# A whole-row first load, two copies on VectorE and new planned landings in a matmul-tanh-multiply kernel

## The chip, the cores and the metric

The kernel runs on one core of one Trainium2 chip. The metric is the device time of one execution in microseconds (us), as the median of several runs.

## The reference

```python
batch, m, k, n = 16, 512, 1024, 768
y1 = np.matmul(x, w1)        # x: (16, 512, 1024) float32, w1 and w2: (1024, 768) float32
y2 = np.matmul(x, w2)
return (np.tanh(y1) * y2).astype(np.float32)
```

Both products share x. Flattened, x has 8192 rows, which are 64 row tiles of 128.

## The kernel before, in words

**Tiling.** Rows go in tiles of 128 (mt 0 to 63). The inner dimension of 1024 is 8 slices of 128 (k), in two halves of 4 (h = 0, 1). The 768 columns of each weight are a block of F = 512 and a block of G = 256; "a" is w1's 512 columns, "b" w2's 512, "g" the 256 columns of both side by side. Operands are cast to float16, products accumulate in float32 in eight PSUM banks.

**Two ways to multiply.** The first four row tiles (HEAD = 4) are multiplied plainly: for each tile and block, eight matmuls m{mt}{s}{k}, for instance m0a0, over the slices in the order in which the weights land. The other 60 tiles go in triples i = 0 to 19. Three tiles by two halves against two halves by three blocks are multiplied with 15 products p0.i to p14.i of four matmuls each; in exchange there are sums of x blocks (S...), of weight blocks (B..., made once) and of partial results (copy, seed, add). Then tanh on ScalarE (t, th) and a product on VectorE (m, mh) give the output. Tile 3 keeps its b block for the end, where its 16 matmuls of 256 columns (m3y...) fill waits of TensorE.

**Getting x transposed.** TensorE needs x with the inner dimension on the partitions. The first seven tiles are transposed on TensorE itself: PT{mt}{h} is four 128 x 128 transposes of one half into a PSUM bank, and e{mt}{h} (evacuate, L383) copies the bank into the float16 tile xT, on ScalarE or VectorE. The halves named in FP32, (0, 0) and (1, 0), are transposed as float32 straight from the loaded tile; the others are first cast to float16 on VectorE, cx{mt}{h} (cast_x). Later tiles are loaded by GpSimd's queue and transposed by DMA from SyncE's queue.

**The first loads.** ScalarE's queue issues a0 to a3, the first four slices of w1 (load_w). SyncE's queue issues, in the order of the list on_sp (L530), the x halves (x00 is half 0 of tile 0), more slices of w1 and then the g slices, each 256 KB. GpSimd's queue issues the b slices and further x tiles (by_pool), behind a gate that waits for the cast cg0 of the first g slice. Casts of weight slices are ca{k} on VectorE, cg0 on VectorE, cg1 to cg7 on ScalarE. The loads of SyncE and ScalarE share eight completion semaphores in turn, so a load is issued only when the one eight places ahead of it has landed.

**What keeps TensorE going at the start.** WARM (L250) is a row of matmuls on constants, issued ahead of everything. FILL is 512 + 512 + 256 columns of the same kind; f0warm and f1warm put one FILL behind PT00 and one behind PT10.

**Who sets the order.** No loop order is written out. Each operation is declared with the engines that may do it and its cost there, a due time, what it needs, and for loads the time at which it will land (lands, LANDING). The class Planner runs these through a list schedule and gives each engine its fixed instruction order; the order of the 15 products (PE_ORDER, strict) is given. So a change of a planned cost, landing or start moves instructions on every engine, all through the kernel. START and P7 (L510, L511) place the triples' products in planned time, lands (L535) and now (L536) the first landings.

**Elsewhere.** D{mt} sums |x| of a tile on ScalarE, for a range flag that is tested at the end (a general path follows if it fails). Stores go out from SyncE's queue, st{mt}; that of tiles 0 and 2 waits for a late product and goes whole, tile 1's in two parts.

Of the kernel before, what the change touches and what calls it, by code (L numbers as in the profile page):

```python
# [74 lines left out]
class Planner:  # L75
# [151 lines left out]
def kernel(  # L227
# [7 lines left out]
    nc = tc.nc  # L235
# [4 lines left out]
    KH = KO // 2  # L240
# [3 lines left out]
    HEAD = 4  # L244
    TRIPLES = (MT - HEAD) // 3
    BY_PE = HEAD + 3
    FP32 = ((0, 0), (1, 0))
    LOW, HIGH = 512.0, 1024.0
    XT_BUFS, XH_BUFS, S_BUFS, O_BUFS, C_BUFS = 12, 8, 2, 9, 2
    WARM = 512, 512, 512, 512, 512, 512, 512  # L250
    FILL = 512, 512, 256
    FREE = 3
    TURNS = (2, 0, 1), (0, 2, 1)
    LANDING = {7: 35.9, 9: 37.2, 8: 39.4, 10: 47.4, 11: 48.3, 12: 49.2, 13: 55.0, 14: 56.3, 15: 57.6}
    rows = list(range(HEAD)) + [HEAD + 3 * i + r for i in range(TRIPLES) for r in (TURNS[i] if i < len(TURNS) else (0, 1, 2))]
    turn = {mt: n for n, mt in enumerate(rows)}
    S_AHEAD, HALVED = 4.0, 4
# [4 lines left out]
    xf = x.flatten_outer_dims().rearrange("(mt p) k -> mt p k", p=P)  # L262
# [8 lines left out]
    banks = [pspool.tile([P, F], f32, name=f"bank{i}") for i in range(8)]  # L271
# [21 lines left out]
    x_first = [early_x[:, mt * K:(mt + 1) * K] for mt in range(HEAD)]  # L293
# [38 lines left out]
    def half(h):  # L332
        return slice(h * KH * P, (h + 1) * KH * P)

    def constants(out, cols):
        fixed = ones.bitcast(bf16)
        pin(nc.tensor.matmul(out[:, :cols], fixed[:, :P], fixed[:, 1:2].to_broadcast([P, cols]), start=True, stop=True))
# [5 lines left out]
    def x_staged(mt, h):  # L343
        return x_first[mt][:, half(h)] if mt < HEAD else arena[:, STAGED * F:(STAGED + 1) * F]

    def load_first(e, mt, h):
        pin(nc.sync.dma_start(x_staged(mt, h), xf[mt][:, half(h)]))

    def cast_x(e, mt, h):
        copy(e, xh(mt)[:, half(h)], x_staged(mt, h))  # L350
# [156 lines left out]
    SLOT = KH * MM  # L507
    CAST = {"a": {"dve": 0.37}, "g": {"act": 0.495}, "g0": {"dve": 0.37}}
    FINE = (5, 36, 37, 45)
    START = 28.6  # L510
    P7 = 13.0  # L511
    ORIGIN = START - 6 * SLOT

    position = {}
# [12 lines left out]

    XX = 1.4
    LAG_FROM, LAG = 21.5, 1.2
    on_sp = "x00 x10 x20 x30 x01 x60 x11 a4 a5 x21 a6 x31 a7".split() + [f"g{k}{t}" for k in range(KH) for t in range(2)]  # L530
    by_pool = "b0 b4 b1 b5 x61 x4 b2 x51 x50 b6 b3 b7".split()
    GATES = {"b0": ("cg0", w_cols("g", 0)[:, :1])}
    arrivals = on_sp[4:] + by_pool
    size = {"x": 0.68, "a": 0.68, "g": 0.75, "b": 0.63}
    lands = dict(zip("x00 a0 x10 a1 x20 a2 x30 a3".split(), (4.31, 4.47, 6.13, 6.53, 7.7, 8.17, 9.05, 9.44)))  # L535
    now = 9.2  # L536
    for n in arrivals:
        now += 1.25 if n in by_pool and n[0] == "x" and len(n) == 2 else size[n[0]]
        lands[n] = now + (LAG if now > LAG_FROM else 0.0)

    for k in range(4):
        op(f"La{k}", {"act": 0.45}, -100, [], load_w, "a", k, issued=[f"La{k - 1}"] if k else [], lands=lands[f"a{k}"])
    for n, what in enumerate(on_sp):
        before = [f"L{on_sp[n - 1]}"] if n else []
        if what[0] == "x":
            op(f"L{what}", {"sp": 0.05}, 0.1 * n - 100, [], load_first, int(what[1]), int(what[2]), issued=before, lands=lands[what])
        else:
            s, k = what[0], int(what[1])
            j = slices.index((s, k))
            js = range(j, j + 1 + (s == "g"))  # L550
            old = [f"c{a}{b}" for a, b in (slices[i - SLOTS] for i in js if i >= SLOTS)] + [f"cx{HEAD + 2}0"] * (STAGED in js)
            op(f"L{what}", {"sp": 0.05}, 0.1 * n - 100, [], load_w, s, k, int(what[2]) if s == "g" else None, issued=before,
               behind=old, lands=lands[what])
    op(f"cx{HEAD + 2}0", {"dve": 0.37}, lands["x60"] - 1, ["Lx60"], cast_x, HEAD + 2, 0,
       behind=[f"cx{m}{h}" for m in range(2, HEAD) for h in range(2) if xh_place(m) == xh_place(HEAD + 2)])
    issued, x_loads = [], {(HEAD + 2, 0): (f"cx{HEAD + 2}0", lands["x60"])}
# [30 lines left out]
    def by_pe(mt, h, due, load):  # L587
        fp32 = (mt, h) in FP32
        op(f"PT{mt}{h}", {"pe": 0.44 if fp32 else 0.24}, due, [load], transpose_pe, mt, h, ("T", mt, h), chains=[("T", mt, h)])
        op(f"e{mt}{h}", {"dve": 0.6 if fp32 else 0.45, "act": 0.5} if mt < HEAD else {"act": 0.5}, due + 0.4, [f"PT{mt}{h}"], evacuate, mt, h, ("T", mt, h),  # L590
           chains=[("T", mt, h)])

    for n, after in enumerate(("PT00", "PT10")):
        op(f"f{n}warm", {"pe": 0.54}, -50, [after], fill, ("f", n), chains=[("f", n)])
    for mt in range(HEAD):
        for h in range(2):
            if (mt, h) not in FP32:
                op(f"cx{mt}{h}", {"dve": 0.37}, lands[f"x{mt}{h}"] - 1, [f"Lx{mt}{h}"], cast_x, mt, h)
            by_pe(mt, h, lands[f"x{mt}{h}"] - 2, f"Lx{mt}{h}" if (mt, h) in FP32 else f"cx{mt}{h}")
        op(f"D{mt}", {"act": 1.05}, START + 8, [f"Lx{mt}0", f"Lx{mt}1"], abs_x, mt, hold=11 + 4 * mt)  # L600
    for mt in rows[HEAD:BY_PE]:
        for h in range(2):
            by_pe(mt, h, x_loads[mt, h][1] - 2 - 0.1 * h * (mt == HEAD + 1), x_loads[mt, h][0])
# [152 lines left out]
    for mt in range(MT):  # L756
        i = (mt - HEAD) // 3 if mt >= HEAD else -1
        if mt < HEAD:
            kept = mt == HEAD - 1
            for t in range(2 if mt == 1 else 0):  # L760
                op(f"st{mt}{'ag'[t]}", {"sp": 0.05}, 1e3, outs[mt][t:t + 1], store, mt, t * F, (F, G)[t], behind=[f"p12.{11 + 2 * mt}"], xfer=0.5)
            if mt != 1:
                op(f"st{mt}", {"sp": 0.05}, 1e3, outs[mt][:1] if kept else outs[mt], store, mt, F if kept else 0, G if kept else N, behind=[f"p12.{11 + 2 * mt}"], xfer=1.0)
            for t in range(2 if kept else 0):
                op(f"st{mt}{chr(88 + t)}", {"sp": 0.4, "act": 0.4}, 2e4, outs[mt][1 + t:2 + t], store, mt, t * G, G, xfer=0.4)
            continue
        late = [f"{('p0', 'p4', 'p11')[(mt - HEAD) % 3]}.{i + 1}"] if i < TRIPLES - 2 else []
        if i == TRIPLES - 1:
            for a, lo, n in ((0, 0, F), (1, F, G)):
                part = outs[mt][a:a + 1]  # L770
                op(f"st{mt}{a}", {"sp": 0.4, "act": 0.4}, 2e4, part, store, mt, lo, n, xfer=0.4)
        else:
            op(f"st{mt}", {"sp": 0.05}, slot_of[max(i, 0), "p2"] + 12, outs[mt], store, mt, behind=late, xfer=1.0)
# [28 lines left out]
    soon = {"L" + n for n in on_sp[:4]} | {f"La{k}" for k in range(4)}  # L802
    pin(nc.vector.memset(ones, 2.0 ** -12))
    for n, cols in enumerate(WARM):
        constants(banks[n], cols)
    for n in sorted(soon, key=lambda n: plan.start_of[n]):
        o = plan.ops[n]
        o["fn"](plan.engine_of[n], *o["args"])
# [107 lines left out]
```

## Time and profile before

| | |
|---|---|
| median of 3 runs | 297.45 us (297.3 to 297.87) |
| profiled execution, its own time | 297.16 us |
| its span in the profile | 295.6 us |
| TensorE busy | 289.5 us |
| VectorE busy | 255.8 us |
| ScalarE busy | 224.4 us |
| GpSimd busy | 42.3 us |
| HBM read, written | 39.85 MB, 25.17 MB |

The span runs from the first recorded instruction to the last; the execution's time has some 1.6 us more around it. In the rows that follow PE is TensorE's matmul side, PEld its weight load, DVE VectorE, ACT ScalarE, POOL GpSimd, SP SyncE; a q behind a name is the engine's instruction queue. A row of the order of time has the start and the duration in us, the engine, the source line, the operation, what it writes and reads, how many were merged (x4), and in brackets how long the engine had been idle and what ended that.

### The profile page before, as it was taken

Reading aid. Unit: us, or ns where it says so; the run is one execution under the profiler, and the core shown is the slowest. Engines: PE = TensorE matmul, PEld = TensorE weight load, DVE = VectorE, ACT = ScalarE, POOL = GpSimd, SP = SyncE. Lnnn points to the kernel's source line nnn. Section 1 sums busy time; section 2 is a strip of 40 time slices with the busy share of each in tenths; the row PEclk is TensorE's granted clock in tenths of the full one; section 3 lists DMA queues with packets and bytes.
Section 4 is the critical chain, followed back from the end, with each engine's and each line's share of the span. In section 5 each row is a group of like instructions: output and inputs, shape, how many; then the busy total and the mean of one; then the engine's idle time right before and its main releaser. Section 6 shows DMA issues by size and latency. Waiting matters only on the chain. (4 is left out here: it accounts for less than half of the span.)

```text
span 295.6 us, 4588 instructions
## 1 busy us (share of the span) xinstructions
PE 289.5 (98%) x1374; PEld 132.3 (45%) x1374; DVE 255.8 (87%) x552; ACT 224.4 (76%) x454; POOL 42.3 (14%) x94
## 2 busy tenths in 40 slices
PE   7999999999999999999999999999999999999994
PEld 3445444444444444444444444444444444444442
DVE  1679999999989998898989888898988889898875
ACT  2698599799878878877888888677777767778442
POOL 0065022202102102202012021020211100000000
PEclk9999999999999999999999999999999999999999
DMA  6999999999999999989999999999999999241234
GB/s 217 391 321 204 182 141 169 210 247 230 240 194 197 247 226 216 252 218 239 204 190 246 231 236 270 164 271 264 224 298 225 213 175 324 104 162 53 109 136 169
DMA packets 84858, 63.63 MB, mean 215 GB/s; under 512 B 62816, under 2 KB 67168, under 8 KB 84832
## 3 DMA queue, kind: packets, MB, share of 16 engines
q1 hardware_dynamic: 73888, 45.10, 59.7%
q0 software_dynamic: 9936, 16.65, 36.0%
q10 hardware_dynamic: 1008, 1.57, 1.5%
q8 instruction: 11, 0.18, 0.2%
q14 instruction: 15, 0.12, 0.1%
HBM read 39.85 MB, written 25.17 MB: 220 GB/s over the span
## 5 line engine op out<-in xcount | busy, mean ns | idle before, releaser
L457 PE MATMUL bank<-b,early_x 128*128 128x512 f16 x640 | 148.3, 379 | 0.0
L457 PEld LDWEIGHTS <-early_x 128*128 128x128 f16 x800 | 78.1, 98 | 94.3 <-DVE early_x L421 0.3
L467 DVE TENSOR_TENSOR bank<-bank,arena 128x512 f32<-128x512 f32 x100 | 69.6, 696 | 13.6 <-ACT arena L461 10.9
L461 ACT ACTIVATE arena<-bank 128x512 f32<-128x512 f32 x100 | 57.6, 596 | 18.1 <-PE bank L457 18.1
L475 DVE TENSOR_TENSOR o<-o,bank 128x256 f32<-128x256 f32 (+1 forms) x128 | 61.9, 516 | 7.3 <-ACT o L470 5.9
L390 ACT ACTIVATE junk<-xh 128x1024 f16<-128x1024 f16 x60 | 63.4, 1057 | 0.1
L457 PEld LDWEIGHTS <-xT 128*128 128x128 f16 x400 | 39.0, 98 | 46.9 <-issue 0.4
L457 PE MATMUL bank<-b,xT 128*128 128x512 f16 x240 | 58.3, 379 | 0.0
L470 ACT ACTIVATE o<-bank 128x256 f32<-128x256 f32 (+1 forms) x80 | 34.8, 438 | 26.0 <-DVE bank L467 22.8
L457 PE MATMUL bank<-wh,xT 128*128 128x512 f16 x160 | 41.0, 379 | 0.0
L457 PE MATMUL bank<-wh,early_x 128*128 128x512 f16 x160 | 40.9, 379 | 0.0
L362 POOL DMA_DIRECT2D xh<-in_x_dram x61 | 32.4, 540 | 16.6 <-ACT junk L390 8.6
L421 DVE TENSOR_TENSOR early_x<-early_x,xT 128x512 f16<-128x512 f16 x80 | 33.5, 420 | 0.5
L470 ACT ACTIVATE o<-arena 128x512 f32<-128x512 f32 x40 | 25.2, 629 | 7.5 <-DVE arena L467 7.5
L501 POOL CAST held<-xT 128x1 f32<-128x1 f16 x18 | 4.5, 251 | 161.3 <-DMA xT<-xh 161.3
L461 ACT ACTIVATE bank<-bank 128x512 f32<-128x512 f32 x40 | 21.4, 570 | 4.7 <-PE bank L457 3.9
L430 PE MATMUL bank<-wh,xT 128*128 128x512 f16 x72 | 19.5, 379 | 0.3
L467 DVE TENSOR_TENSOR arena<-bank,arena 128x512 f32<-128x512 f32 x20 | 13.7, 686 | 3.6 <-ACT arena L461 3.6
L421 DVE TENSOR_TENSOR early_x<-xT,xT 128x512 f16<-128x512 f16 x40 | 16.7, 418 | 0.0
L421 DVE TENSOR_TENSOR early_x<-xT,early_x 128x512 f16<-128x512 f16 x40 | 16.7, 418 | 0.0
L467 DVE TENSOR_TENSOR bank<-arena,bank 128x512 f32<-128x512 f32 x20 | 13.8, 692 | 0.1
L390 ACT ACTIVATE junk<-wh 128x768 f16<-128x768 f16 x16 | 13.6, 847 | 0.1
(51 smaller groups left out, 140.0 us busy)
## 6 DMA issues: line engine op xcount, KB each, us to landing
out_dram<-o SPq DMA_DIRECT2D x59, 384.0 KB, 5.1
xh<-in_x_dram POOLq DMA_DIRECT2D x58, 256.0 KB, 6.7
arena<-in_w_dram SPq DMA_DIRECT2D x12, 256.0 KB, 5.6
early_x<-in_x_dram SPq DMA_DIRECT2D x8, 256.0 KB, 4.9
arena<-in_w_dram ACTq DMA_DIRECT2D x4, 256.0 KB, 5.9
wh<-in_w_dram POOLq DMA_DIRECT2D x8, 128.0 KB, 5.5
xT<-xh SPq DMA_TRANSPOSE x57, 4.2
out_dram<-o SPq DMA_DIRECT2D x3, 256.0 KB, 2.5
```

The lines of the kernel that those rows point to most:

```text
L362: pin(nc.gpsimd.dma_start(xh(mt)[:, cols], xf[mt][:, cols]))
L390: pin(nc.scalar.activation(junk[:, :src.shape[-1]], src, ACT.Abs, scale=scale, accum_out=sums[:, column:column + 1]))
L421: pin(engine[e].tensor_tensor(x_operand(i, v), x_operand(i, a), x_operand(i, b), OP[how]))
L430: pin(nc.tensor.matmul(bank(chain)[:, :rhs.shape[-1]], xt(mt)[:, k, :], rhs, start=first, stop=k == KO - 1, skip_group_check=True))
L457: pin(nc.tensor.matmul(place(i, dst), x_operand(i, a)[:, k, :], w_rhs(b, k), start=begins and k == 0, stop=k == KH - 1, skip_group_check=T ...
L461: pin(nc.scalar.activation(place(i, dst), place(i, src), ACT.Copy, scale=float(sign)))
L467: pin(nc.vector.tensor_tensor(place(i, dst), a, b, ALU.add if signs == (1, 1) else ALU.subtract))
L470: pin(nc.scalar.activation(out_tile(HEAD + 3 * i + r)[:, lo:lo + n], place(i, src)[:, :n], ACT.Tanh, scale=float(sign)))
L475: pin(nc.vector.tensor_tensor(o, o, place(i, src)[:, at:at + n], ALU.mult))
L501: pin(nc.gpsimd.tensor_copy(held, xt(mt)[:, 0, :1]))
```

## The change

- Tile 0 of x is loaded by one DMA in whole rows (x0, 512 KB) instead of the halves x00 and x01; x01's place in the list of SyncE's loads falls away.
- WARM becomes nine matmuls of 512 columns and one of 128, and wraps over the eight banks. The fill behind PT00 goes, the one behind PT10 stays.
- The planned landings of the first eight loads are replaced, those of the rest are counted on from a later base with one load fewer. START, P7 and four entries of LANDING are lowered by 0.1 to 0.5.
- The copy e20 may go only to VectorE; for the other copies of the first four tiles ScalarE's planned cost is 0.6 instead of 0.5.
- Tile 0's store becomes two stores, like tile 1's.

The order that comes out of the planner: PT01 stands right behind PT00, with its cast first on VectorE; e01 and e20 are VectorE's, e31 ScalarE's; D1, D2 and D3 stand later on ScalarE, D1 behind cg7; cg4 stands ahead of tha0; m0g5 stands one place earlier. Between 30 and 280 us TensorE's order is the same, while adds and multiplies of VectorE and some copies and tanhs of ScalarE trade places. In the last triple p5, p4, p13 and p14 stand ahead of the first piece of tile 3's b block, and on VectorE the add60 ahead of the last but one triple's mh0. GpSimd's order is the same.

```diff
-    WARM = 512, 512, 512, 512, 512, 512, 512
+    WARM = 512, 512, 512, 512, 512, 512, 512, 512, 512, 128
-    LANDING = {7: 35.9, 9: 37.2, 8: 39.4, 10: 47.4, 11: 48.3, 12: 49.2, 13: 55.0, 14: 56.3, 15: 57.6}
+    LANDING = {7: 35.9, 9: 37.2, 8: 39.0, 10: 47.2, 11: 48.1, 12: 49.0, 13: 55.0, 14: 56.3, 15: 57.6}
...
     def load_first(e, mt, h):
-        pin(nc.sync.dma_start(x_staged(mt, h), xf[mt][:, half(h)]))
+        if h is None:
+            pin(nc.sync.dma_start(x_first[mt], xf[mt]))
+        else:
+            pin(nc.sync.dma_start(x_staged(mt, h), xf[mt][:, half(h)]))
...
-    START = 28.6
-    P7 = 13.0
+    START = 28.4
+    P7 = 12.5
...
-    on_sp = "x00 x10 x20 x30 x01 x60 x11 a4 a5 x21 a6 x31 a7".split() + [f"g{k}{t}" for k in range(KH) for t in range(2)]
+    on_sp = "x0 x10 x20 x30 x60 x11 a4 a5 x21 a6 x31 a7".split() + [f"g{k}{t}" for k in range(KH) for t in range(2)]
...
-    lands = dict(zip("x00 a0 x10 a1 x20 a2 x30 a3".split(), (4.31, 4.47, 6.13, 6.53, 7.7, 8.17, 9.05, 9.44)))
-    now = 9.2
+    lands = dict(zip("x0 a0 x10 a1 x20 a2 x30 a3".split(), (4.65, 4.87, 6.2, 6.55, 7.92, 8.12, 9.25, 9.45)))
+    now = 9.5
     for n in arrivals:
         now += 1.25 if n in by_pool and n[0] == "x" and len(n) == 2 else size[n[0]]
         lands[n] = now + (LAG if now > LAG_FROM else 0.0)
+    lands["x00"] = lands["x01"] = lands["x0"]
...
-        op(f"e{mt}{h}", {"dve": 0.6 if fp32 else 0.45, "act": 0.5} if mt < HEAD else {"act": 0.5}, ...
+        op(f"e{mt}{h}", {"dve": 0.45} if (mt, h) == (2, 0) else {"dve": 0.6 if fp32 else 0.45, "act": 0.6} if mt < HEAD else {"act": 0.5}, ...
...
-    for n, after in enumerate(("PT00", "PT10")):
-        op(f"f{n}warm", {"pe": 0.54}, -50, [after], fill, ("f", n), chains=[("f", n)])
+    op("fwarm", {"pe": 0.54}, -50, ["PT10"], fill, ("f", 0), chains=[("f", 0)])
...
-            for t in range(2 if mt == 1 else 0):
+            for t in range(2 if mt < 2 else 0):
...
-            if mt != 1:
+            if mt > 1:
...
-        constants(banks[n], cols)
+        constants(banks[n % len(banks)], cols)
```

More of the change, by code (lines that the diff above doesn't have):

```diff
@@ L545 @@
         if what[0] == "x":
-            op(f"L{what}", {"sp": 0.05}, 0.1 * n - 100, [], load_first, int(what[1]), int(what[2]), issued=before, lands=lands[what])
+            op(f"L{what}", {"sp": 0.05}, 0.1 * n - 100, [], load_first, int(what[1]), int(what[2]) if what[2:] else None, issued=before, lands=lands[what])
         else:
@@ L589, in by_pe, with x_load @@
         op(f"PT{mt}{h}", {"pe": 0.44 if fp32 else 0.24}, due, [load], transpose_pe, mt, h, ("T", mt, h), chains=[("T", mt, h)])
-        op(f"e{mt}{h}", {"dve": 0.6 if fp32 else 0.45, "act": 0.5} if mt < HEAD else {"act": 0.5}, due + 0.4, [f"PT{mt}{h}"], evacuate, mt, h, ("T", mt, h),
+        op(f"e{mt}{h}", {"dve": 0.45} if (mt, h) == (2, 0) else {"dve": 0.6 if fp32 else 0.45, "act": 0.6} if mt < HEAD else {"act": 0.5}, due + 0.4, [f"PT{mt}{h}"], evacuate, mt, h, ("T", mt, h),
            chains=[("T", mt, h)])
-    for n, after in enumerate(("PT00", "PT10")):
-        op(f"f{n}warm", {"pe": 0.54}, -50, [after], fill, ("f", n), chains=[("f", n)])
+    def x_load(mt, h):
+        return f"Lx{mt}" if f"x{mt}" in on_sp else f"Lx{mt}{h}"
+    op("fwarm", {"pe": 0.54}, -50, ["PT10"], fill, ("f", 0), chains=[("f", 0)])
     for mt in range(HEAD):
@@ L597 @@
             if (mt, h) not in FP32:
-                op(f"cx{mt}{h}", {"dve": 0.37}, lands[f"x{mt}{h}"] - 1, [f"Lx{mt}{h}"], cast_x, mt, h)
-            by_pe(mt, h, lands[f"x{mt}{h}"] - 2, f"Lx{mt}{h}" if (mt, h) in FP32 else f"cx{mt}{h}")
-        op(f"D{mt}", {"act": 1.05}, START + 8, [f"Lx{mt}0", f"Lx{mt}1"], abs_x, mt, hold=11 + 4 * mt)
+                op(f"cx{mt}{h}", {"dve": 0.37}, lands[f"x{mt}{h}"] - 1, [x_load(mt, h)], cast_x, mt, h)
+            by_pe(mt, h, lands[f"x{mt}{h}"] - 2, x_load(mt, h) if (mt, h) in FP32 else f"cx{mt}{h}")
+        op(f"D{mt}", {"act": 1.05}, START + 8, sorted({x_load(mt, h) for h in range(2)}), abs_x, mt, hold=11 + 4 * mt)
     for mt in rows[HEAD:BY_PE]:
```

## The prediction

> **What bounds the kernel now.** I read the page's busy times first, then PE's waits, then the windows, then the order of time in three places: the first 10 us, the stretch from 17 to 25 us, the last 12 us.
>
> ```profile
> PE 289.5 (98%) x1374; PEld 132.3 (45%) x1374; DVE 255.8 (87%) x552; ACT 224.4 (76%) x454; POOL 42.3 (14%) x94
> ```
> ```profile
> PE bank L337 <- DVE ones L803: 1.3, 1, 1.3
> PE bank L380 <- DMA early_x<-in_x_dram: 0.2, 1, 0.2
> ```
> ```profile
> 4.60:6.33 1.73, 1.52 (x7) 1.04 (x8) 0.43 (x1) 0.59 (x1) 0.00 (x0) 1.00 0.88 300
> 6.33:9.54 3.21, 3.05 (x17) 1.44 (x18) 1.41 (x4) 1.17 (x2) 0.00 (x0) 1.00 1.05 405
> 31.40:283.97 252.57, 252.57 (x1172) 114.44 (x1172) 228.41 (x489) 200.06 (x409) 33.15 (x72) 1.00 0.99 210
> ```
>
> (In the windows the columns are the stretch, its length, the busy time of PE, PEld, DVE, ACT and POOL, the granted clock, the DMA share and GB/s.) PE is the bound and it never rests: the list of its waits holds 1.5 us, all before 5 us, and in the window from 31.40 to 283.97 it is busy for the whole 252.57 us. Products and their order there are nearly untouched by the change. So the time is PE's start, plus a fixed stream, plus what is lost before 31 us and after 284 us. Only the two ends can pay.
>
> A busy PE hides short waits, because a matmul's shown time is longer than its step: in the rows of the end below, eight 512-column matmuls start at 286.37 and the next instruction at 288.10, so one step is 0.216 us. I therefore read starts, not busy times.
>
> ```profile
> 1.30 3.17 PE L337 MATMUL bank<-ones 128*128 128x512 bf16 x7 [1.30 <-DVE ones L803]
> 4.67 0.98 PE L380 MATMUL bank<-ident,early_x 128*128 128x128 f32 x4 [0.21 <-DMA early_x<-in_x_dram]
> 5.49 0.71 PE L337 MATMUL bank<-ones 128*128 128x512 bf16 x3
> 6.33 0.39 PE L430 MATMUL bank<-wh,xT 128*128 128x512 f16 x1
> 6.56 0.60 PE L380 MATMUL bank<-ident,early_x 128*128 128x128 f32 x4
> 6.99 0.71 PE L337 MATMUL bank<-ones 128*128 128x512 bf16 x3
> 7.54 0.90 PE L430 MATMUL bank<-wh,xT 128*128 128x512 f16 x3
> 8.47 0.40 PE L380 MATMUL bank<-ident_h,xh 128*128 128x128 f16 x4
> 17.43 0.38 PE L430 MATMUL bank<-wh,xT_kept 128*128 128x512 f16 x1
> 17.66 0.59 PE L430 MATMUL bank<-wh,xT 128*128 128x512 f16 x2
> 24.62 1.67 PE L430 MATMUL bank<-wh,xT 128*128 128x512 f16 x7
> ```
> ```profile
> 4.73 0.43 DVE L368 CAST wh<-arena 128x512 f16<-128x512 f32 x1 [2.92 <-DMA arena<-in_w_dram]
> 5.69 0.59 ACT L366 CAST xT<-bank 128x512 f16<-128x512 f32 x1 [1.53 <-PE bank L380]
> 7.98 0.43 DVE L368 CAST xh<-early_x 128x512 f16<-128x512 f32 x1 [0.74 <-DMA early_x<-in_x_dram]
> 15.98 0.42 DVE L368 COPY xT_kept<-bank 128x512 f16<-128x512 f16 x1
> 17.18 0.43 DVE L368 CAST wh<-arena 128x512 f16<-128x512 f32 x1 [0.78 <-DMA arena<-in_w_dram]
> ```
>
> What to see: the head is a chain from landing to cast to PE. The first g slice is cast at 17.18 as it lands and is ready at 17.61; its matmul m0g0 starts at 17.66. The four fp32 transposes take 0.82 us the first time (4.67 to 5.49) and 0.43 the second (6.56 to 6.99); the 1280-column fill takes 0.55 (6.99 to 7.54). So PE's real speed doubles between 4.7 and 5.5 us, though the granted clock shows 1.00 all along.
>
> **The landings.** The kernel's old planned landings can be set beside the rows: x20 at 7.7 against a cast at 7.98, a0 at 4.47 against 4.73. The rows are 0.27 later. With this offset the new plan means x0 at 4.92, a0 5.14, x10 6.47, x20 8.19, a2 8.39; and since x01's place is gone while its base is 0.3 later, everything after a3 comes 0.68 - 0.30 = 0.38 earlier. This is the plan's claim, not the trace's. The bytes are the same, so the gain must come from the ramp:
>
> ```profile
> DMA packets 645, 1.19 MB, mean 187 GB/s; under 512 B 64, under 2 KB 64, under 8 KB 645
> DMA packets 726, 1.32 MB, mean 405 GB/s; under 512 B 80, under 2 KB 80, under 8 KB 726
> ```
>
> The first row covers 0 to 6.37 us, the second 6.37 to 9.64. Once running, 405 GB/s is full pace; 0.38 us at that pace is 0.15 MB more out of a ramp that moved 1.19 MB. That is possible with fewer, longer rows. Bounds: no more bytes, so no gain after a3 (0), and 0.68. I take 0.38, inside both.
>
> **Head, step by step.** WARM is nine 512s and a 128, 9.25 steps at half speed (2 x 0.216 = 0.43), from 1.30 to about 5.25. So the first transposes PT00 move from 4.67 to 5.25: a loss of 0.58 that x0's landing (4.92) does not force. The first fill is gone (0.55 back). PT00 then takes 0.43 to 0.82; I take 0.55, as the speed doubles within it: 5.80. e00 on ACT follows 0.20 after (5.49 to 5.69) and lasts 0.59, so m0a0 starts at 6.64, not 6.33. PT01 (0.23) runs in that hole; its cast, 4.92 to 5.36, is early enough. PT10 6.86, fill to 7.84, m0a1 7.84 (was 7.54). PT20 waits x20's cast, 8.19 + 0.43: 8.67 (was 8.47). m2a0 waits PT20 and e20, now 0.42 on DVE instead of 0.59: 9.57, where the old kernel stood at 9.54. From there to m0g0 both run 30 steps of 0.216 (6.48), and five groups of transposes of 0.23 in the new order, six in the old (PT01 is done). New: 9.57 + 6.48 + 1.15 = 17.20, and about 0.2 of waits for casts that land 0.38 earlier: 17.40. Old: 17.66. Head gain 0.26. DVE's two added copies less the moved e31, 0.42 net, lie in its idle time before landings (0.74 ahead of 7.98, 0.78 ahead of 17.18); without that cover they would cost 0.42 on every later cast.
>
> **ACT, which is late next.** In the new order D1 leaves the front, and tha0 moves behind cg4.
>
> ```profile
> 17.17 0.62 ACT L366 CAST wh<-arena 128x512 f16<-128x512 f32 x1
> 17.69 1.08 ACT L433 ACTIVATE o<-bank 128x512 f32<-128x512 f32 x2
> 18.68 1.14 ACT L366 CAST wh<-arena 128x512 f16<-128x512 f32 x2
> 19.72 0.59 ACT L433 ACTIVATE o<-bank 128x512 f32<-128x512 f32 x1
> 20.21 1.12 ACT L366 CAST wh<-arena 128x512 f16<-128x512 f32 x2
> 21.72 1.14 ACT L366 CAST wh<-arena 128x512 f16<-128x512 f32 x2 [0.39 <-DMA arena<-in_w_dram]
> 22.77 1.05 ACT L390 ACTIVATE junk<-early_x 128x1024 f16<-128x1024 f32 x1
> ```
>
> Starts differ by 0.52 for a cast and 0.49 for a tanh. New: cg4 16.80 (17.18 - 0.38), two tanh, cg1 18.30, cg5 18.82, ready 19.44. m0g5 is now the second matmul of its group, 9 steps after m0g0: 19.34. It waits 0.15. Then tanh, cg2, cg6, tanh, cg3 21.36, cg7 21.88, D1 22.40: all ahead of PE and 0.37 ahead of before. So m0b0 starts at 24.46 instead of 24.62: 0.16 of the 0.26 is left. POOL's b loads start behind cg0, so 0.38 earlier. The changed place of D3, ahead of e40, ends about 27.65, and PT51 now waits for e40: the margin is under 0.1 us, and each tenth that ACT is late there is a tenth lost.
>
> **SP.** One load fewer is issued, and x60's now waits for a0's landing instead of x01's; six loads of 256 KB, x10 to a3, are then still on their way, so I take 0. Tile 0's store becomes two issues at about 176 us; PE's full window above covers it: 0, at worst the price of one issue, 0.4 us of SP.
>
> **The end.** The planner moves p4, p13 and p14 of the last triple ahead of the first filler (m3y0), and add60 ahead of mh0 on DVE.
>
> ```profile
> 283.97 0.27 PE L430 MATMUL bank<-wh,xT_kept 128*128 128x256 f16 x1
> 284.08 1.03 PE L457 MATMUL bank<-b,early_x 128*128 128x512 f16 x4
> 285.50 1.04 PE L457 MATMUL bank<-b,early_x 128*128 128x512 f16 x4
> 286.37 1.89 PE L457 MATMUL bank<-wh,early_x 128*128 128x512 f16 x8
> 288.57 1.89 PE L457 MATMUL bank<-b,xT 128*128 128x512 f16 x8
> ```
> ```profile
> 284.21 0.42 DVE L475 TENSOR_TENSOR o<-o,bank 128x256 f32<-128x256 f32 x1 [0.20 <-ACT o L470]
> 284.74 0.70 DVE L467 TENSOR_TENSOR bank<-bank,arena 128x512 f32<-128x512 f32 x1
> ```
>
> From 283.97 to p3's start at 288.57 are 4.60 us for four products (16 x 0.216 = 3.46) and eight fillers of 256 columns (8 x 0.108 = 0.86): 0.28 of waits. In the new order add60 can start near 284.2, when p0 is out, so p4 waits only to 284.92 (0.09), and p3's seed is ready before the fillers end: p3 at 288.38. Gain 0.19; bounds 0.28 (no wait) and 0 (add60 late as before).
>
> **Sum.** Profiled execution 297.16 (span 295.6 and 1.56 around it): 297.16 - 0.16 - 0.19 = 296.81. The median of the runs is 297.45, 0.29 above that execution; on it the forecast is 297.1. Differences below 0.2%, 0.6 us, are about what a measurement of this kernel can tell from no change.
>
> **Rivals.**
> Larger gain: the ramp speeds up by the upper bound (0.68), the casts stop binding PE, the 0.35 of waits I left in the head goes, and the end gives 0.28. Then 0.16 + 0.35 + 0.28 = 0.8: 296.65. For it: PE is work-bound once data is there. Against: 0.58 lost ahead of PT00 stays.
> No gain: the landings after a3 do not move. m0g0 then waits for cg0 at 17.61 as now, early stalls and the longer WARM eat part of the end's 0.19: 297.4.
> Slower: the clock. Before, PE was nearly always fed from 1.30 on, and doubled its speed about 4 us later. In the new kernel a hole of about 0.6 us with only 0.23 us of fp16 transposes in it follows PT00, where a dense fill stood. If the doubling comes only after 7 us, the gain is gone; if it comes at about 9.5 us, PT00 costs 0.27 more, PT01 0.2, PT10 0.43, the fill 0.55, PT20 0.23 and seven matmuls 7 x 0.216 = 1.51, in all 3.2, of which the waits that the new order leaves there (about 1.0: 0.6 behind e00, 0.3 for PT20 and m0a2, 0.1 for m1a0) and an estimated 0.6 of waits for casts up to m0g0 hide 1.6: +1.6 - 0.35 = +1.2, 298.6. Against it: in the trace the doubling fell beside transposes and after a pause of PE (the 0.21 wait at 4.67).
> The Trainium skill ("TensorE: Matmul & The Clock Gate", Part 1: The HAM clock gate, and Part 4: PE-mode transpose) says that the speed rises after a busy window of about 3.4 us that runs free of the kernel's start, and that transposes do not count as busy in the same way. The 4 us from 1.30 to the doubling agree with the first; no row here shows the second. By it alone the sum would be the slower case's 298.6, and that case likelier than I make it.
>
> **Chances.** Forecast (-0.1 to -0.8 us) 0.50, of it 0.20 beyond 0.6 us; larger gain 0.22, all but 0.01 beyond; no gain 0.12; slower 0.16, all but 0.01 beyond. So faster 0.41, same 0.44, slower 0.15. The forecast's own range is 296.6 to 297.4; the range with the larger gain, the lost gain and the mild part of the slower case is 296.5 to 297.9.
>
> **What would show it.** In the new profile: PT00 near 5.25 and m0a0 near 6.64; m0g0 near 17.40 with cg0's cast near 16.80; a short wait before m0g5; m0b0 near 24.46; p3 of the end 0.19 earlier against p0 than now. I am wrong if cg0's cast is still at 17.18, if the second group of fp32 transposes takes over 0.5 us, or if PE shows waits between 25 and 284 us.

## The result, and the profile after

Forecast was 297.1 us, a gain of 0.35. The changed kernel takes 297.78 us (median of 14 runs, 297.31 to 298.99) against 297.35 for the kernel before (14 runs beside it): ratio 1.002 [1.001, 1.0029], 0.43 us slower. Run again it was 297.81 against 297.3, ratio 1.0007 [0.999, 1.0024], an interval that by itself does not exclude no change. (Medians are of all runs; ratios and intervals leave out single executions that are slowed by over 1.5%.)

Its profiled execution took 297.8 us, 0.64 more than that of before. From the two traces: the last triple's p0 starts 0.45 later (283.56 against 283.11), from there to TensorE's end 0.10 less is used, the last store is out 0.03 later after that, and the span ends 1.66 us behind the last data packet instead of 1.40, 0.26 more. Between the head and the end nothing changed: from the first triple's p6 (31.86 against 31.40) to that p0 it is 251.70 against 251.71. So the loss is in the head and behind the last store, and the new order at the end brought a part of what was forecast.

First the page's busy times and PE's list of waits, as shown of before:

```profile
PE 289.2 (98%) x1374; PEld 132.3 (45%) x1374; DVE 254.8 (86%) x553; ACT 223.9 (76%) x453; POOL 42.8 (14%) x94
```
```profile
PE bank L337 <- DVE ones L809: 1.3, 1, 1.3
PE bank L433 <- DVE xT L371: 0.5, 1, 0.5
PE bank L433 <- DVE wh L371: 0.4, 1, 0.4
PE bank L383 <- DVE xh L371: 0.3, 1, 0.3
```

PE is as full as before. The 0.2 in front of PT00 is gone (the longer warm-up covers it); in its place stand waits for the copies of tile 0, for the cast of a2 and for the cast of x31. (Of the copies m0a0 itself needs e00, on ScalarE until 6.42; the list names VectorE, because e01 there ended last, at 6.48.) They are shown where they stand in the order of time of after:

```profile
5.17 0.63 PE L383 MATMUL bank<-ident,early_x 128*128 128x128 f32 x4
6.48 0.39 PE L433 MATMUL bank<-wh,xT 128*128 128x512 f16 x1 [0.45 <-DVE xT L371]
7.72 0.90 PE L433 MATMUL bank<-wh,xT 128*128 128x512 f16 x3
8.66 0.40 PE L383 MATMUL bank<-ident_h,xh 128*128 128x128 f16 x4
9.42 1.02 PE L433 MATMUL bank<-wh,xT 128*128 128x512 f16 x4 [0.36 <-DVE wh L371]
15.53 0.40 PE L383 MATMUL bank<-ident_h,xh 128*128 128x128 f16 x4 [0.32 <-DVE xh L371]
17.93 1.24 PE L433 MATMUL bank<-wh,xT 128*128 128x512 f16 x5
24.98 1.24 PE L433 MATMUL bank<-wh,xT 128*128 128x512 f16 x5
```

Up to PT20 (8.66) everything is where the forecast put it. m0g0 (17.93) and m0b0 (24.98) are 0.53 and 0.52 later than forecast. VectorE's casts of a2, of x31 and of the first g slice in after, and below them that of x31 in before, show why:

```profile
8.94 0.43 DVE L371 CAST wh<-arena 128x512 f16<-128x512 f32 x1 [0.34 <-DMA arena<-in_w_dram]
15.05 0.43 DVE L371 CAST xh<-early_x 128x512 f16<-128x512 f32 x1 [0.93 <-DMA early_x<-in_x_dram]
17.34 0.43 DVE L371 CAST wh<-arena 128x512 f16<-128x512 f32 x1 [1.14 <-DMA arena<-in_w_dram]
```
```profile
14.91 0.43 DVE L368 CAST xh<-early_x 128x512 f16<-128x512 f32 x1 [0.25 <-DMA early_x<-in_x_dram]
```

All wait for a DMA. The cast of the g slice starts at 17.34; it was 17.18 before and 16.80 in the forecast. That of x31 starts at 15.05; it was 14.91 before, and 0.38 earlier, as forecast, would be 14.53.

It is x31 that sets m0g0 here, not the g slice itself. The transposes PT31 wait for x31's cast (the 0.32 ahead of 15.53), and from there TensorE runs without a pause through ten matmuls to m0g0 at 17.93; cg0 has by then been ready for 0.16 (17.77). In before PT31 (15.48) does not wait, and m0g0 follows cg0 (17.61) by 0.05. So of the 0.27 that m0g0 is later than before, 0.14 is the later landing of x31, and the rest comes from the new order, in which PT31 stands one matmul further ahead of m0g0.

Three profiled executions below (noload, oldplan_split, dvepad) hold a stall of TensorE of 2 to 4 us at 102 or 163 us that most executions of these kernels lack. Of these only rows ahead of the stall are used, and distances between rows behind it.

### The profile page after: what moved, and what is told of

It reads as the page before. It is cut to its first block, busy times and chain, and to the rows that moved or that the text cites. A ratio compares the mean times of both kernels' runs of the same rounds, so it can differ in the third digit from the quotient of the medians.

```text
span 296.3 us, 4578 instructions
## 1 busy us (share of the span) xinstructions
PE 289.2 (98%) x1374; PEld 132.3 (45%) x1374; DVE 254.8 (86%) x553; ACT 223.9 (76%) x453; POOL 42.8 (14%) x94
## 3 DMA queue, kind: packets, MB, share of 16 engines
q10 hardware_dynamic: 1008, 1.57, 1.5%
## 5 line engine op out<-in xcount | busy, mean ns | idle before, releaser
L504 POOL CAST held<-xT 128x1 f32<-128x1 f16 x18 | 5.1, 284 | 165.3 <-DMA xT<-xh 165.3
L464 ACT ACTIVATE bank<-bank 128x512 f32<-128x512 f32 x40 | 21.5, 567 | 2.2 <-PE bank L460 1.3
L424 DVE TENSOR_TENSOR early_x<-xT,early_x 128x512 f16<-128x512 f16 x40 | 16.7, 418 | 0.0
L424 DVE TENSOR_TENSOR early_x<-xT,xT 128x512 f16<-128x512 f16 x40 | 16.7, 418 | 0.0
L470 DVE TENSOR_TENSOR arena<-arena,bank 128x512 f32<-128x512 f32 x20 | 13.6, 681 | 0.0
```

Source lines behind the costliest of these rows:

```text
L424: pin(engine[e].tensor_tensor(x_operand(i, v), x_operand(i, a), x_operand(i, b), OP[how]))
L464: pin(nc.scalar.activation(place(i, dst), place(i, src), ACT.Copy, scale=float(sign)))
L470: pin(nc.vector.tensor_tensor(place(i, dst), a, b, ALU.add if signs == (1, 1) else ALU.subtract))
L504: pin(nc.gpsimd.tensor_copy(held, xt(mt)[:, 0, :1]))
```

## The experiments

### The same two kernels again, and the order on ScalarE

**ctl_before, ctl_after** (the two kernels unchanged):

> The kernel before again, unchanged, for a second profile. If the late packets that the profile of the changed kernel shows between 12 and 14 us come and go by themselves, the landings here need not equal the first profile's: x31 at 14.89 us and the first part of g0 cast at 17.18 us may move by up to 0.5 us. If they belong to the new loads, this profile repeats the first one within 0.1 us.

> The changed kernel again, unchanged. Theory A (ScalarE's order: D2 and D3 stand before e40, so the second late group of transposes waits): e40 starts at least 1.5 us after e61 starts, PT51 waits for it, and the time is again 0.3 to 0.6 us above before, whatever the landings do. Theory B (the new loads land late by themselves): x31 lands after 14.9 us again, cg0's cast starts at 17.2 us or later. Theory C (the late packets of the first profile were chance): x31 lands near 14.5 us, cg0's cast starts near 16.8 us.

Measured: 297.08 for the one run of before, 297.81 for after. In the second trace of after the first g slice lands at 17.46 instead of 17.24, its cast starts at 17.56 and m0g0 at 18.16; the span again ends 1.65 behind the last data packet (before 1.37). So both losses come again.

**e31dve**:

> The changed kernel with the copy e31 left to VectorE as before. The planner then puts D1 back at about 15 us, D2 behind cg7 and D3 ahead of e61, and changes nothing else but m1a7's place by some matmuls. Theory A: e40 starts right behind PT40, PT51 no longer waits for it, and the time falls 0.3 to 0.7 us below the changed kernel, to 0.0 to 0.4 us below before. Theory B: it stays within 0.15 us of the changed kernel.

```diff
-{"dve": 0.45} if (mt, h) == (2, 0) else ...
+{"dve": 0.45} if (mt, h) in ((2, 0), (3, 1)) else ...
```

With e31 on VectorE the planner puts D1 at 15 us, D2 behind cg7 and D3 ahead of e61, so D3 is no longer ahead of e40. 297.74 us, ratio 1.0012 [0.9998, 1.0026]; m0g0 17.99, m0b0 25.01, p6 of the first triple 31.77 (after 31.86). From m0b0 to p6 that is 6.76, and in the repeat of after, with D3 still ahead of e40, it is 6.76 as well (25.20 to 31.96). So the thin margin of PT51 behind e40 cost nothing and is not the cause.

### How tile 0 is loaded

**halves, rows64, rows_only** (two half-row loads back to back; two loads of 64 whole rows; the kernel before with the whole-row load and the new first landings alone):

> The changed kernel with tile 0 loaded by two DMAs of half rows, one right behind the other, instead of one in whole rows; every engine's order stays, one more load is issued. If the whole rows speed up the first landings, PT00 starts 0.2 to 0.6 us later here and the landings after a3 come 0.2 to 0.4 us later, and the time rises by 0.1 to 0.4 us over the changed kernel. If the rows' length does nothing, landings and time stay within 0.1 us of it.

> The changed kernel with tile 0 still in whole rows, but as two DMAs of 64 rows each; every engine's order stays. Theory R, row length (4 KB reads throw the queues out of step): slow packets as in the changed kernel, g01 at 17.2 to 17.5 us, time within 0.2 us of it. Theory R, size of the one transfer (512 KB in one issue): the slow packets are gone as with two half-row loads (14 against 23 to 37), g01 lands at 16.8 us, and the time falls by 0.2 us or more.

> The kernel before with tile 0 in whole rows and the new planned landings, without the other parts (WARM 7 with both fills, old costs of the copies, START, P7, LANDING and tile 0's store as before). The planner moves ScalarE's D1 and two casts as it does in the changed kernel. Theory R (the whole rows bring slow packets, and the later loads lose what the ramp gained): a few tens of 2 KB packets take over 140 ns between 7 and 15 us, g01 lands after 17.1 us, and the time is 0.2 to 0.6 us above before. Theory P (the slow packets were chance; the planner's new order costs): fewer than ten slow packets, g01 near 16.7 us, the time still 0.2 us or more above before. If both are wrong, g01 lands at 16.7 us and the time is 0.1 to 0.4 us below before.

```diff
 halves
-            pin(nc.sync.dma_start(x_first[mt], xf[mt]))
+            for t in range(2):
+                pin(nc.sync.dma_start(x_staged(mt, t), xf[mt][:, half(t)]))
 rows64
+            for t in range(2):
+                pin(nc.sync.dma_start(x_first[mt][t * 64:(t + 1) * 64], xf[mt][t * 64:(t + 1) * 64]))
 rows_only: load_first, on_sp, lands and now of after in the kernel before
```

halves: 297.95, ratio 1.0021 [1.0006, 1.0036]. x10 lands only at 7.86, so m0a1 is at 8.94 (after 7.72), but the first g slice lands at 16.81, 0.4 ahead of after, where 0.2 to 0.4 later was expected. TensorE cannot use that: it comes to m0g0 only at 18.24 (after 17.93), and by p6 it is about level again (31.92 against 31.86). rows64: 301.48, ratio 1.013 [1.0113, 1.0147], far above both expectations; PT00 starts only at 8.13. rows_only: 297.91, ratio 1.0032 [1.0007, 1.0057]. Its order of time shows what the slower rival of the prediction feared, a late doubling of TensorE's speed, though not in after:

```profile
5.17 1.09 PE L383 MATMUL bank<-ident,early_x 128*128 128x128 f32 x4 [0.71 <-DMA early_x<-in_x_dram]
6.05 1.27 PE L337 MATMUL bank<-ones 128*128 128x512 bf16 x3
7.12 0.63 PE L383 MATMUL bank<-ident_h,xh 128*128 128x128 f16 x4
7.97 1.06 PE L383 MATMUL bank<-ident,early_x 128*128 128x128 f32 x4
```

Behind a pause of 0.71 us PE stays at half speed (a group of fp32 transposes 1.06 where after has 0.63 as shown above) until about 9 us, and m0g0 is at 18.89. The longer warm-up of the change fills that pause; in after the speed doubled at 4.7, inside the warm-up (the starts of its 512-column matmuls are 0.43 apart up to 4.69 and 0.22 behind it). That the pause is the reason is not shown: warm7 below pauses for 0.6 ahead of PT00 at 5.03 and is at full speed by 7.03. And a late doubling need not cost anything: in oldplan below, with no pause there, it came between 6.4 and 7.2, m0a1 was at 8.17 instead of 7.72, and m0g0 came no later behind x31 than in after.

### Planned times

**oldplan** (the planned start, landings and base of before under the new load):

> The kernel after with the planned start of the triples, the later planned landings and the base of the landings after a3 put back to what the old plan had (so everything after a3 is planned 0.38 later); the whole-row load, the longer warm-up, the copies and the stores as changed. Theory L (the landings themselves are late, whatever the plan says): the last g half of slice 0 lands near 17.3, m0g0 starts 17.8 to 18.0, time 297.6 to 297.9. Rival P (an order made for landings that do not come costs the time): with an order for later landings PE recovers, m0b0 near 24.6, time 297.2 to 297.4.

```diff
-    START = 28.4
-    P7 = 12.5
+    START = 28.6
+    P7 = 13.0
-    now = 9.5
+    now = 9.88
 (and LANDING as before)
```

298.7, ratio 1.0044 [1.003, 1.0057], though TensorE's last product is where it was before (291.03). Two things came together. The g slice landed early in this execution (16.90; m0g0 17.60), so the head says nothing against the plan of after: in oldplan, after and its repeat m0g0 follows that landing by 0.70, 0.69 and 0.70, and the landing of x31 (14.70, 15.03 and 15.26) by 2.90 in all three. And the end lost 1.3 us, which led to the next runs.

### Blocks of code that are fetched during the last store

**warm7, warm7_split, oldplan_split** (the warm-up cut back to 7 x 512; the same columns in ten matmuls; oldplan with two matmuls more for the same columns):

> The changed kernel with seven warming matmuls instead of ten, all else as it is; PE is then idle from about 4.5 us until x0 lands at 5.0 us. If the longer WARM delays PT00 (the prediction's 0.58), PT00 moves earlier by 0.1 us or more. Since x0 landed at 5.04 and PT00 started at 5.17, I expect no change of PT00 and the doubling of PE's speed to fall later by up to 0.5 us; time 0 to 0.3 us above the changed kernel. If the clock needs unbroken work, the doubling falls after 6 us and the time rises by over 0.5 us.

> The kernel after with a warm-up of 7 x 512 columns, cut into ten matmuls, so that TensorE's code has as many instructions as after; columns, orders and all else as in the kernel with seven. There the last block of TensorE's code was fetched at 294.0, within the last store, and the store came 1.3 later. Theory C: the fetch goes back to about 288, time 298.0 to 298.7 (the stall at 163 us, 0.8, stays) or 297.5 (if that was chance). Rival: time stays at 299.4 or more.

> The kernel with the old planned times (whole-row load, long warm-up and copies as changed), with two more matmuls in the warm-up for the same 4736 columns, so every later instruction of TensorE is four places further on in its code. Theory C: in the kernel with the old planned times the head is as good as before (last product of TensorE 291.03) and 1.3 us are lost at the end, because a 16 KB block of instructions is fetched at 293.2 on one of the 16 DMA engines that still write the last store; four instructions more move that fetch to about 288, the last store is out 3.2 after TensorE's end, time 297.1 to 297.4. Rival (the end is late for another reason): fetch or not, time stays at 298.4 to 298.8.

```diff
 warm7
+    WARM = 512, 512, 512, 512, 512, 512, 512
 warm7_split
+    WARM = 512, 512, 512, 512, 256, 256, 256, 256, 256, 256
 oldplan_split
+    WARM = 512, 512, 512, 512, 512, 512, 512, 256, 256, 256, 256, 128
```

warm7: 299.87, ratio 1.0098 [1.0074, 1.0123]; expected was at most 0.3 above after. warm7_split: 297.72, ratio 1.002 [1.0005, 1.0035]. oldplan_split: 297.78, ratio 1.0008 [0.9982, 1.0034], where oldplan had 1.0044; expected was 297.1 to 297.4. Columns and orders are those of the kernels without the split. The DMA view of 292 to 298 us shows what moved; it has GB/s in 40 slices, then the queue that carries the 16 KB block. warm7, then warm7_split:

```profile
GB/s 0 0 0 0 0 0 287 369 369 355 369 287 375 444 321 307 301 355 151 41 61 7 14 14 27 20 27 20 14 0 0 0 0 0 0 0 0 0 0 0
...
q8 instruction: 1, 0.02, 0.9%
```
```profile
GB/s 0 109 396 382 341 382 328 335 355 321 348 321 369 294 75 68 0 0 0 0 0 0 0 0 0 0 0 0 55 0 0 0 0 0 0 0 0 0 0 0
```

In warm7 the last store does not end with the rest: for 1.4 us some 20 GB/s trickle, about a sixteenth of the 350 or so before. That fits one of the 16 DMA engines that had first to fetch 16 KB of instructions (at 294.0, 0.88 us long); the trace does not name the engine. The last data packet is out 4.17 us behind TensorE's end, in oldplan 4.18 (fetch at 293.2), in warm7_split 2.91 (fetch at 287.9), in before 2.88 (fetch at 286.6). These fetches come every 22 to 32 us, once for about 250 instructions of TensorE. That such a fetch costs 1.3 us when it falls into the last store is shown by the pair warm7 and warm7_split, and by oldplan; in after it falls clear (288.0). The rest of warm7's excess is at 163 us, where ScalarE waits 1.5 us for a store and TensorE loses about 0.5; the second kernel's profile lacks this. The late doubling in warm7 is not the reason: m0g0 is at 17.70 in both kernels.

**dvepad** (twelve small instructions more on VectorE at the start):

> The kernel after with twelve instructions of one column more on VectorE at the start, where it is idle, into a spare tile. In after VectorE has 699 instructions against 714, and an 8 KB block of instructions is fetched at 294.59, behind the last store on its DMA engine, in front of the store's completion; before it was fetched at 291.66. If it is VectorE's block that is fetched when its 704th instruction comes near: fetch at about 291.7 to 292, the span ends 1.35 after the last store instead of 1.65, time 297.5. Rival (another engine's code, or no cost): fetch stays at 294.6, time 297.7 to 297.9.

```diff
+    spare = once.tile([P, 12], f32, name="spare")
+    for n in range(12):
+        pin(nc.vector.memset(spare[:, n:n + 1], 0.0))
```

After fetches an 8 KB block at 294.59, exactly as the last data packet ends, and the span then ends later than in before. The DMA view of after from 294.3 to 295.3:

```profile
GB/s 288 205 123 41 82 0 41 41 0 41 0 328 0 0 0 0 0 0 0 0 0 0 0 0 0 0 0 0 0 0 0 0 0 0 0 0 0 0 0 0
...
q14 instruction: 1, 0.01, 1.9%
```

In dvepad VectorE has 711 instructions instead of 699, and the block is fetched as its 704th comes up, 0.62 behind TensorE's end instead of 2.91. So whose code it is came out as expected. The gain did not: from TensorE's end to the end of the span it is 4.61 us against 4.57 in after (the last data packet is now later, 3.04 behind TensorE's end instead of 2.91), and 4.28 in before, where the block was fetched 0.33 behind TensorE's end. The time is 298.01, and 297.48 over the nine of its 13 runs that the ratio uses, as expected; but that ratio, 1.0006 [0.9994, 1.0018], does not tell it from after. So that the block costs after its 0.26 is not shown by this run. For it speaks a comparison of all profiles: in the seven that fetch this block as the last data packet ends, the span ends 1.65 to 2.03 behind that packet, in the other thirteen 1.31 to 1.74, eleven of them at most 1.57. Dvepad's head, however, is the most telling of all the runs:

```profile
16.80 0.43 DVE L371 CAST wh<-arena 128x512 f16<-128x512 f32 x1 [1.11 <-DMA arena<-in_w_dram]
17.29 1.24 PE L433 MATMUL bank<-wh,xT 128*128 128x512 f16 x5
24.44 1.46 PE L433 MATMUL bank<-wh,xT 128*128 128x512 f16 x6
```

The forecast said 16.80, 17.40 and 24.46. With the orders of after and these landings (x31 at 14.37, the g slice at 16.71), the head does what was predicted.

### The slow packets

The trace has each packet of the loads. A 2 KB packet takes 84 ns and a 1 KB packet some 50; between 7 and 16 us some take 140 to 1000 ns. **dummy** adds a useless load at x01's old place, **late01** moves x01 behind a7 in the kernel before:

> The kernel after with one load more, of no use: the second half of tile 0 once more, into free space, at the place in the list where x01 stood; every engine's order is that of after. It costs 256 KB, some 0.65 us, of each later landing. If the slow packets come with the whole rows of the first load: over 14 packets above 140 ns between 7 and 16 us as in after, first g slice landed near 17.9, time 298.2 to 298.5. If they come because the loads behind x30 run one place earlier: at most 5, x60 near 10.9, first g slice near 17.5, time 297.9 to 298.2.

> The kernel before with the load x01 moved behind a7, so x60 to a7 come one place earlier, as in the changed kernel, but with no whole-row load and not with both halves of tile 0 at the start. PE has to wait for PT01, planned 0.75 later at m0g0: time 297.8 to 298.3. If the slow packets (over 140 ns, 7 to 16 us) come because the loads after x30 run early: 14 or more, as in every kernel with the whole rows. If they come with tile 0's 512 KB at the start (one load of whole rows or both halves at once): at most 5, as in every kernel with the half at its old place, and x60 lands near 10.1.

```diff
 dummy: load_first for x01
+            to = early_x[:, HEAD * K:HEAD * K + F] if (mt, h) == (0, 1) else x_staged(mt, h)
 late01
-"x00 x10 x20 x30 x01 x60 x11 a4 a5 x21 a6 x31 a7"
+"x00 x10 x20 x30 x60 x11 a4 a5 x21 a6 x31 a7 x01"
```

dummy: 298.55 (one run), 34 slow packets, the first g slice at 17.74. late01: 299.46, ratio 1.0076 [1.0045, 1.0106], slower than expected (a wait of 1.23 at 32.6 us was not foreseen), with 12 slow packets, between the two answers. Over all profiles: with the half x01 at its old place 0, 5, 0, 4, 0 and, in noload_split, 18; with tile 0's 512 KB at the start 14 to 37 in thirteen. So they go with the early 512 KB nearly always, but not with it alone; what makes them is open. They go with late landings too: among these thirteen the two with the least packet time above the usual, halves and dvepad (3.0 us each, after 6.8), have the earliest landings of the first g slice (16.81 and 16.71).

### The rest of the change without the load

**noload, noload_split** (after with the two half loads and old landings; the same with the split warm-up):

> The kernel after with only the load undone: tile 0 in two half-row loads at their old places in the list, with the old planned landings; the longer warm-up, one fill, the copies and the stores as changed. Theory L: the landings are those of before (x60 10.8, first g slice 17.05), at most 5 packets over 140 ns between 7 and 16 us, m0g0 17.6 to 17.8, time 297.2 to 297.4. Rival W (the longer warm-up, with PT00 0.5 later, is what costs): m0g0 17.9 to 18.1 with the landings of before, time 297.6 to 297.9.

> The kernel with only the load undone (tile 0 in two halves at the old places, the old planned landings; long warm-up, one fill, copies and stores as changed), its warm-up cut into two matmuls more for the same columns. Theory C: the 1.7 us that the kernel without the split lost were the block of TensorE's code falling on the last store (its head was as good as before: m0b0 24.57) and, in its profile, a stall at 163 us; with the split: fetch near 288, time 297.2 to 297.5. Rival W (the longer warm-up or the new order of the copies costs the time): 298.5 or more.

```diff
-"x0 x10 x20 x30 x60 ..."
+"x00 x10 x20 x30 x01 x60 ..."
 (lands and now as before; noload_split: WARM as oldplan_split)
```

299.17, ratio 1.0077 [1.0054, 1.01], and 298.65, ratio 1.0045 [1.003, 1.0061]; expected was 297.2 to 297.5. Here my theory missed. In noload's profile, of an execution of 303.48 us with the stall at 163, the head is as good as before (m0g0 17.62, m0b0 24.57). In noload_split's a load at the end of the list is late, as ScalarE's row for cg3 and cg7 shows:

```profile
22.97 1.14 ACT L369 CAST wh<-arena 128x512 f16<-128x512 f32 x2 [0.96 <-DMA arena<-in_w_dram]
```

The last g half landed at 22.95, when GpSimd's b loads had begun, instead of some 21.5; m0b0 came at 25.66. The same is seen in oldplan_tail (23.10). Whether it befalls most runs of this order is not shown, so what the warm-up and the copies cost by themselves stays open. That they cost something is a rival which these two runs do not exclude.

### The end alone, and the version that came out

**tail, tailwarm, oldplan_tail** (the kernel before with the first filler behind p14; the same with 256 columns more of warm-up; the new load with old planned times, split warm-up and that end):

> The kernel before with the end alone in the new order: the first filler waits for p14 instead of p0, so p5, p4, p13 and p14 of the last triple and add60 move ahead; nothing else moves. By the prediction's sum p3 of the last triple starts 0.19 us (bounds 0 and 0.28) earlier against p0, and the time falls by 0.1 to 0.2 us. The changed kernel's profile gave 5.36 us from p0.19 to p3.19 against 5.46: 0.10. The rival: stores and copies at the end take the gain back, 0 within 0.05 us.

> The kernel before with the new order at the end (the first filler behind p14) and 256 columns more of warm-up, which end at about 4.55, where x00 lands. If the pause ahead of PT00 is what lets PE's speed double late in some executions (7.1 us with the new end alone, 5.1 to 5.45 in two of before): doubling by 5.5, PT00 4.7, m0g0 near 17.66, time 296.9 to 297.1. If the pause does not matter: PT00 0.05 to 0.1 later, m0g0 17.7 to 17.9, time 297.1 to 297.3, no better than the new end alone.

> As the kernel with the old planned times and the split warm-up, and the first filler of the last triple behind p14. If the head recovers with the old planned times, the end's order adds 0.1 and the code fetch falls clear of the last store: TensorE's end 290.9, time 296.9 to 297.2, the best of both. If one of the three fails: 297.4 or more.

```diff
 tail, tailwarm, oldplan_tail
-FILLERS = "p0", "p3"
+FILLERS = "p14", "p3"
 tailwarm
+    WARM = 512, 512, 512, 512, 512, 512, 512, 256
```

tail 297.13 against 297.39, ratio 0.9998 [0.9973, 1.0022]; tailwarm 297.01 against 297.14, ratio 0.9999 [0.9989, 1.001]; oldplan_tail 297.65, ratio 1.0014 [1.0001, 1.0026]. In all three p0 to p3 of the last triple takes 5.35, in before 5.46: 0.1 us for the end's order, less than the runs can tell. The 256 columns did not make PE's speed double by 5.5, as one answer had it (its first fp32 transposes still take 1.09). No version beats before beyond its interval; before with the new end is level with it.

## Why the prediction was wrong, point by point

For the profiled execution the forecast was 296.81, and 297.80 came, 0.99 more. The rows divide it, but for rounding: m0b0 is 0.52 late, 0.10 is lost from m0b0 to p6, 0.09 of the gain at the end did not come, and 0.29 stands behind TensorE's end. The first of the prediction's signs of being wrong, a cast of cg0 still at 17.18, is there (17.34); the second group of fp32 transposes takes 0.47, and PE's list of waits shows none behind 25 us.

**The landings: the step that failed.** The prediction let everything after a3 land 0.38 earlier than in before; x31 and the first g slice landed 0.14 and 0.15 later. The ramp was right, and more than right: 1.38 MB instead of 1.19 by 6.37 us, where 0.15 MB more was forecast. These are the DMA views of after for the two windows that the prediction shows of before, and for 9.64 to 16.7 us those of before and after:

```profile
DMA packets 603, 1.38 MB, mean 217 GB/s; under 512 B 56, under 2 KB 56, under 8 KB 603
```
```profile
DMA packets 713, 1.30 MB, mean 397 GB/s; under 512 B 80, under 2 KB 80, under 8 KB 713
```
```profile
GB/s 395 383 383 383 418 383 406 360 348 360 383 406 406 371 418 395 395 371 383 383 383 383 395 383 406 383 383 377 354 366 366 360 354 348 348 354 342 354 348 348
DMA packets 1808, 2.66 MB, mean 377 GB/s; under 512 B 161, under 2 KB 859, under 8 KB 1808
```
```profile
GB/s 371 383 418 395 395 371 395 395 383 418 395 383 395 395 395 371 360 313 279 267 313 313 325 337 319 313 337 360 360 377 331 360 377 389 377 371 371 360 377 383
DMA packets 1795, 2.56 MB, mean 363 GB/s; under 512 B 160, under 2 KB 927, under 8 KB 1795
```

Of the lead of 0.19 MB, 0.02 is lost in the second window and 0.10 in the third, where the rate dips to 267 GB/s: 23 slow packets, 6.8 us of packet time too much, 0.43 us on each of 16 engines if it were spread evenly. It is not, as the completions show. A load of 256 KB reports 16 of them, one for each engine, and the cast waits for the last. In before the last one of the first g slice comes 0.62 behind the first, at 17.09; in after 1.10, at 17.24; in its repeat 1.42, at 17.46; in dvepad, with 14 slow packets, 0.81, at 16.71. The middle one of the 16 is at 16.72 before and 16.42 in after: on most engines 0.30 of the forecast 0.38 was there, and the last three come from 16.96 on. Nor was after one bad draw: in the eleven profiles with the 512 KB at the start (dummy, with its load more, and rows64 left out) the first g slice lands from 16.71 to 17.46, with the median at 17.10; in the six with x01 at its old place from 16.97 to 17.27, with the median at 17.06. By the medians, too, there was no gain. The prediction reckoned a landing by bytes and mean rate, and it is set by the slowest engine. (The Trainium skill, "DMA: Bandwidth & Descriptors", section "Why a DMA increments its semaphore by 16 and not by 1", says that the engines finish independently and that only the full 16 mean that all data landed; the traces agree, with the spreads just given.)

**Head, the chain itself: right.** PT00 5.17 (forecast 5.25), m0a0 6.48 (6.64), m0a1 7.72 (7.84), PT20 8.66 (8.67). m2a0 9.85 instead of 9.57, since a2 landed 0.5 after the plan. m0g0 17.93 instead of 17.40: x31's landing, 0.52 late against the forecast (15.03 instead of 14.89 - 0.38 = 14.51). With x31 at 14.51 the 2.90 found above would have given 17.41. The sum reached its 17.40 another way, by 0.2 of waits spread over all casts, so that the two agree so well is in part luck.

**ACT: right.** m0g5 waits 0.15 as forecast; from m0g0 to m0b0 it is 7.05 instead of 6.96, forecast 7.06. From m0b0 to p6 it is 6.88 instead of 6.78, so the head's 0.36 at m0b0 became 0.46 at p6. That is not the margin of D3 and e40, but a wait for a load of GpSimd's queue, as the row of the weight load there says:

```profile
26.38 0.22 PEld L383 LDWEIGHTS <-xh 128*128 128x128 f16 x4 [0.44 <-DMA xh<-in_x_dram]
```

The six matmuls from 24.98 take 1.30, and the transposes start 0.10 behind them; in the repeat, with the same order, this wait is missing.

**SP: 0, and nothing showed.** **The end: size off.** p4 waits 0.10 (forecast 0.09), but p13 waits 0.07 too, which the sum left out: 0.10 instead of 0.19. What was not in the sum at all is the 0.26 behind the last store.

**The rivals.** The no-gain case came nearest (landings after a3 not earlier, cast at 17.18 as before): 297.4 against 297.78, the rest being about the 0.16 of the cast and the 0.26 behind the last store. The larger gain needed the landing. The slower one did not occur in after; that TensorE's speed can double as late as it feared is what rows_only shows. By the rule of the Trainium skill there ("TensorE: Matmul & The Clock Gate", Part 1: The HAM clock gate), a busy stretch of about 3.4 us doubles the speed. After doubles 3.4 us behind its first matmul and agrees; rows_only doubles about 4 us behind its pause, but other executions do not fit: the repeat of after doubles at most 2.8 us behind its first matmul, oldplan at least 5.1, warm7 at most 2.0 behind its pause. Where the two differ, the measured moments hold.

## What to carry to other kernels

A load has landed when the slowest of its 16 DMA engines is done: forecast it from the last completion and the spread of several executions, not from bytes over mean rate, and take one profile's landing as one draw. A new order can also put another load on the path: here x31's, which the old order had off it. That the earlier planned times by themselves cost anything is not shown (oldplan's head keeps the same distances from the landings). And where a change of a few instructions moves the time by about 1 us, look for instruction blocks among the last stores before explaining it by the work.

## What was not expected of the hardware

- Blocks of instructions are fetched among the data's packets: 16 KB of TensorE's code in front of a last store's packets cost 1.3 us of it, and two or three more instructions in the warm-up moved it away (warm7 299.87, warm7_split 297.72).
- Single 2 KB packets of loads took up to 1.0 us instead of 84 ns, and in different places from one execution of the same kernel to the next (12.3 to 14 us in after, 10.3 to 11 in its repeat).
- In two profiles the tail of SyncE's last load came 1.4 us late, among GpSimd's first loads (22.95 and 23.10 instead of some 21.5).
